# Constant products ahead of the first turn, one column tile, block 2's and 3's squares at other slices, FFN1's first left sums seven slices later

## The chip, the cores and the metric

The kernel runs on one core of one Trainium2 chip. The metric is the device time of one execution in microseconds (us). Before the change three runs took 2862.64, 2865.20 and 2865.36 us (median 2865.2). One execution was also recorded by the hardware profiler, instruction by instruction; every number about single instructions comes from that record, and its times count from the first instruction.

The engines are called as in the profile: PE (matrix products), PEld (its weight loads), DVE (vector), ACT (scalar and activation), POOL (general), SP (which issues DMAs). Each works through its own queue in the order in which it was written; an instruction that waits holds everything behind it on the same engine.

## What is computed

One layer of a transformer-like trunk: 2048 tokens of 1024 numbers, float32. Shift, scale and gate come from a conditioning vector c.

```python
mod_all = einsum('bd,lde->lbe', silu(c), ada_w) + ada_b
h = rms_norm(x, g0) * (1 + sc_m) + sh_m
y = stick_breaking_mixer(h, w_qkv, w_o)      # 16 heads of 64, causal, blocks of 128
x = x + gt_m * rms_norm(y, g1)
h = rms_norm(x, g2) * (1 + sc_f) + sh_f
g, u = split(h @ w_in); y = (silu(g) * u) @ w_out   # width 2816
x = x + gt_f * rms_norm(y, g3)
```

The mixer computes, per head, z = q k^T / 8, a weight for every earlier position as the product of sigmoid(z) with all sigmoid(-z) between, and the weighted sum of the values.

## The kernel before, in words

Float32 products are made of three fast ones: every operand is split into a high part (a cast on ACT, or POOL) and a low part (the difference, on DVE or POOL), and `mm3` (lines 176 to 180) multiplies high by high, high by low and low by high.

**Order.** PE, ACT, DVE and POOL run in the order in which the program is written; SP's DMAs are ordered by the framework. The unit of the order is a slice: one call of `mm3`, three products of 512 columns. The 2048 tokens are four blocks of 512, the 16 heads eight pairs. The projections are a list of steps, `STEPS`: pair 0 with block 0, pair 1 with block 0 (parked in memory), then pair 0 with blocks 1, 2, 3, and so on. A step has a key product (t = 1), a query product (t = 0) and a value product (t = 2), each of eight slices k = 0 to 7, then two empty slices. Step 2 is pair 0, block 1; step 3 is pair 0, block 2.

**The start** (lines 774 to 937, written out by hand). The first 2 x 1024 modulation numbers come in eight tiles m of 128, shift and scale each. A tile's `ada` weights are loaded by `row_load(m)`. Tiles 0 and 1 are multiplied on PE (`column`, line 699: eight products of one column per half, into `acol`); tiles 2 to 7 on DVE (`row_sum`, line 707: weights times `c_rows` with a running sum), where `c_rows` is silu(c) spread over all partitions by two products of a constant matrix. `row_done` (line 715) adds the bias. Block 0's x is normed by rows (`x_square`, `x_scale`), turned by PE (`turn_x`), modulated on ACT (`full`), split (`high`, `low`) and multiplied at once for pairs 0 and 1 (`products`).

**Blocks 1 to 3 of x** come already turned (`cols_load`), four loads of 512 KB each. Block 1's norm is taken from rows. For blocks 2 and 3, `cols_square` (line 315) squares the four loads on ACT, `cols_add` (line 323) adds them on DVE, m = 1, 2, 3 and a closing add of 512; for block 3 all squares from m = 1 on use the same buffer, so each waits for the add before it. `cols_sum` (line 330) sums over partitions with four products of one column and makes the root on POOL; `x_spread` (line 343, DVE) and `x_share` (line 350: four turns on PE, then a copy on ACT to the tile `xv`) lay the scales out as a row. `first_norm` (line 406) then scales (`scale_cols`; odd tiles on POOL), modulates and splits tile by tile, and stores each pair of tiles (1024 KB, `h_s`). In `project` (line 443) the tables `XSQUARE_AT`, `XADD_AT`, `XSUM_AT` say at which slice of the step before each of these is written. In step 2 this is block 2's work, in step 3 block 3's.

**Attention** starts in step 2's value product: `score` on PE into three banks (`z`), two sigmoids on ACT, `break_sticks` on DVE and POOL, turns on PE, `split_high` on ACT, `split_low` on DVE, and the product with the values. Its slots alternate with projection slices.

**FFN1** (lines 1531 to 1580): 44 groups, two halves of the tokens by 22; a group is seven products of four slices, a Strassen-like scheme. The left matrices of a group are sums of raw weights, made in the group before: `left_add` (line 1331, DVE) and `left_split` (line 1345, ACT and DVE). `ADD_AT` and `SPLIT_AT` give their slices; for the group after groups 0 and 22, where the right matrices of a half are still being split as well, `ADD_LATE` and `SPLIT_LATE` do, counted from the start of group 0 or 22. `taken` (line 1482) reads each product from its bank; line 1498 adds product 7 into `up1`, and product 4 goes on in the same bank after that. Raw weights of a group are loaded two groups ahead (`left_load`), into the buffers of the group that was just split.

Of the kernel before, what the change touches and what calls it, by code (L numbers as in the profile page):

```python
# [9 lines left out]
F32 = mybir.dt.float32  # L10
# [28 lines left out]

COLUMNS = 2  # L40

# [65 lines left out]
def hybrid_trunk_kernel(  # L107
# [215 lines left out]
    def cols_add(b, m):  # L323
        total = x_squares[b][0]
        if m < KC // 2:
            nc.vector.tensor_tensor(total, total, x_squares[b][m], op=ALU.add)
        else:
            nc.vector.tensor_tensor(total[:, 0], total[:, 0], total[:, 1], op=ALU.add)
# [21 lines left out]
    def x_share(b):  # L350
        spread = x_spreads.pop(b)
        pool, tag = (tps, "t") if b < 2 else (accps, "acc")
        pt = pool.tile([P, BT], F32, name=f"xr{b}", tag=tag)
        for i in range(4):
            nc.tensor.transpose(pt[:, i * P : (i + 1) * P], spread[:, i], ident)
        x_row[b] = att.tile([P, BT], F32, name=f"xv{b}", tag="tmp", bufs=BUFS["tmp"])
        nc.scalar.copy(x_row[b], pt)

    def x_scale(i):
        nc.vector.tensor_scalar(x_norm[i], x_tiles.pop((0, i)), x_rstd.pop((0, i)), None, op0=ALU.mult)  # L360
# [82 lines left out]
    def project(at):  # L443
# [10 lines left out]
        def product(t):  # L454
# [7 lines left out]
            for k in range(KC):  # L462
                if t == 1:
                    if p == 0:
                        first_norm(b, k + (4 if b == 1 else 3))
                    if k in (3, 5) and waiting:
                        waiting.pop(0)()
                if nb == 2 and (t, k) == (1, 4):
                    cols_load(3)
                if nb:  # L470
                    if (t, k) in XSQUARE_AT[nb]:
                        cols_square(nb, XSQUARE_AT[nb][t, k])
                    if (t, k) in XADD_AT[nb]:
                        cols_add(nb, XADD_AT[nb][t, k])
                    if (t, k) in XSUM_AT[nb]:
                        (cols_sum, x_spread, x_share)[XSUM_AT[nb].index((t, k))](nb)
                if (t, k) in NORM_AT:
# [207 lines left out]
    def row_load(m):  # L685
# [9 lines left out]
        for seg in range(2):  # L695
            src = ada_cols_first[m, seg] if m < COLUMNS else ada_rows[m - COLUMNS, seg]
            nc.sync.dma_start(halves_of[seg], src)
# [17 lines left out]
    def row_done(m):  # L715
        total = acol[:, 2 * m : 2 * m + 2] if m < COLUMNS else sums.pop(m)
        nc.vector.tensor_tensor(mod[:, :, m], total, b_cols[:, 0:2, m], op=ALU.add)
# [29 lines left out]
    def turn_x(m):  # L747
        turned_x[m] = x_turn(m)
# [25 lines left out]
    first_h, first_full, stores, turned_x = norm_h[0], {}, [], {}  # L774
    acol = zps.tile([P, BT], F32, name="acol", tag="z")
    c_line = att.tile([P, D], F32, name="c_line", tag="qkn", bufs=BUFS["qkn"])
# [25 lines left out]
    c_spread = [zps.tile([P, BT], F32, name=f"cs{half}", tag="z") for half in range(2)]  # L802
    c_halves = [slice(half * BT, (half + 1) * BT) for half in range(2)]
    for half in range(2):
        nc.tensor.matmul(c_spread[half], ones, c_line[:, c_halves[half]], start=True, stop=True)
    column(0, 0)
    column(0, 1)
    x_square(0, 0)
    for i in range(1, 4):
        x_square(0, i)  # L810
        x_scale(i - 1)
    c_rows = att.tile([P, D], F32, name="c_rows", tag="qkn", bufs=BUFS["qkn"])
    for half in range(2):
        nc.scalar.activation(c_rows[:, c_halves[half]], c_spread[half], AF.Sigmoid)
    x_scale(3)
# [3 lines left out]
    row_done(0)  # L819
    weights_high(0, 1)  # L820
# [3 lines left out]
    low(0)  # L824
    for half in range(2):
        nc.vector.tensor_tensor(
            c_rows[:, c_halves[half]], c_spread[half], c_rows[:, c_halves[half]], op=ALU.mult
        )
    products(0, 0, 1)
    column(1, 0)  # L830
# [10 lines left out]
    turn_x(2)  # L841
    products(0, 0, 2)
    weights_low(1, 1)
    for t in (1, 0, 2):
        first_acc[1, t] = zps.tile([P, BT], F32, name=f"pj1_0_{t}", tag="z")
    products(1, 0, 1)
    low(1)
    row_sum(2, 0)
    weights_high(1, 0)
    row_sum(2, 1)  # L850
    row_done(2)
    products(0, 1)
    weights_low(1, 0)
    products(1, 1, 1)
    full(2)
    high(2)
    weights_high(1, 2)
    products(1, 0, 0)
    row_sum(3, 0)
    weights_low(1, 2)  # L860
    turn_x(3)
    products(1, 1, 0)
    low(2)
    x_load(1, 0)
    x_load(1, 1)
# [900 lines left out]
```

## Time and profile before

| | |
|---|---|
| runs | 2862.64, 2865.20, 2865.36 us |
| profiled execution | 2863.12 us, span 2860.8 us |
| mean granted PE clock | 0.992 of full speed |
| PE busy | 2803.4 us of the span |
| DVE, ACT, POOL busy | 2032.0, 1633.3, 1284.1 us |
| FFN1's products | 1583.3 to 2433.0 us |

A line of the timeline has the start in us, the length in us, engine, line of the kernel, operation, what it writes and reads, its shape, and in brackets the idle time of the engine before it and what ended that. A window has busy time and number of instructions of each engine, the clock that PE was granted (1.00 is full), the share of time in which the 16 DMA engines were busy, and GB/s. A group has count, busy time and mean ns of one, then idle time before. L178, L179 and L180 are the three products of `mm3`, wherever they are called from.

### The profile page before, as it was taken

What the parts mean: (1) busy time and instruction counts of PE and PEld (TensorE: products, weight loads), DVE (VectorE), ACT (ScalarE), POOL (GpSimd) and SP (SyncE); (2) the same over time, 40 slices, a digit from 0 to 9 for tenths busy, and PEclk for the clock granted to TensorE, in tenths of its full rate; (3) what the DMA queues carried; (4) which work ended last, traced back from release to release, by engine and by line L of the source; (5) the groups of instructions that cost most, each with busy time, mean ns of one, the idle gap of its engine ahead of it and who ended that gap; (6) DMA issues with size and microseconds to landing.
All of it is one profiled execution on the core that took longest, in us unless ns stands there. A gap on an engine that the chain in (4) does not pass through costs nothing.

```text
span 2860.8 us, 41725 instructions
## 1 busy us (share of the span) xinstructions
PE 2803.4 (98%) x13809; PEld 2339.3 (82%) x13809; DVE 2032.0 (71%) x2827; ACT 1633.3 (57%) x3269; POOL 1284.1 (45%) x2030
## 2 busy tenths in 40 slices
PE   8799999999999999999999999999999999999998
PEld 7588888888888888887887888888788888888887
DVE  6788888888888888888866866555776655134376
ACT  5587777788787777877644533333433333322233
POOL 0475666667576665656410222212222222644454
PEclk8899999999999999999999999999999999999999
DMA  9665547666576545637289645334554335545566
GB/s 361 233 227 162 169 159 239 190 194 225 168 233 200 173 149 174 202 119 247 63 306 307 212 139 158 109 93 152 158 164 120 111 95 174 190 132 153 181 214 199
DMA packets 239209, 518.94 MB, mean 181 GB/s; under 512 B 22417, under 2 KB 108433, under 8 KB 222098
## 3 DMA queue, kind: packets, MB, share of 16 engines
q1 hardware_dynamic: 238994, 516.28, 55.8%
q8 instruction: 109, 1.79, 0.3%
q14 instruction: 106, 0.87, 0.1%
HBM read 348.95 MB, written 118.49 MB: 163 GB/s over the span
## 4 chain that ended last, share of the span: by engine, by line
PE 87%; DVE 4%; ACT 2%; issue 1%; DMA 1%; POOL 1%; SPq 0%; DVEq 0%; POOLq 0%; ACTq 0%
PE s L178 9%; PE s L180 9%; PE s L179 9%; PE z L588 8%; PE o L667 8%; PE t L639 8%; PE pj L178 5%; PE pj L180 5%; PE pj L179 5%; PE o L180 5%; PE o L178 5%; PE o L179 5%; PE y L180 2%; PE y L178 2%; PE y L179 2%
## 5 line engine op out<-in xcount | busy, mean ns | idle before, releaser
L629 POOL TENSOR_TENSOR a<-a,w 128x512 f32<-128x512 f32 (+3 forms) x640 | 622.2, 972 | 220.4 <-DVE w L622 130.9
L622 DVE TENSOR_TENSOR_SCAN w<-z,c,begin 128x512 f32<-128x512 f32 x384 | 489.2, 1278 | 83.6 <-ACT z L607 61.8
L178 PE MATMUL s<-r,l 128*128 128x512 f32 x1232 | 481.6, 391 | 4.7 <-DVE p L1498 4.4
L180 PE MATMUL s<-r,l 128*128 128x512 f32 x1232 | 479.5, 389 | 0.0
L179 PE MATMUL s<-r,l 128*128 128x512 f32 x1232 | 479.4, 389 | 0.0
L605 ACT ACTIVATE a<-z 128x512 f32<-128x512 f32 (+3 forms) x640 | 347.0, 542 | 168.3 <-PE z L588 136.8
L667 PE MATMUL o<-aT,v 128*128 128x512 f32 (+3 forms) x1280 | 385.0, 382 | 0.1
L655 DVE TENSOR_TENSOR aT<-t,aT 128x512 fp32r<-128x512 f32 (+3 forms) x640 | 358.5, 594 | 25.8 <-ACT aT L649 25.3
L588 PE MATMUL z<-kt,qt 128*128 128x512 f32 (+3 forms) x1280 | 363.9, 365 | 0.0
L649 ACT CAST aT<-t 128x512 fp32r<-128x512 f32 (+3 forms) x640 | 313.8, 533 | 79.6 <-PE t L639 69.6
L607 ACT ACTIVATE z<-z 128x512 f32<-128x512 f32 (+3 forms) x640 | 345.4, 540 | 0.0
L1506 POOL TENSOR_TENSOR one<-p,p 128x512 f32<-128x512 f32 x44 | 70.9, 1611 | 577.6 <-issue 320.6
L178 PE MATMUL pj<-ht,w 128*128 128x512 f32 x768 | 310.9, 405 | 4.8 <-issue 1.4
L639 PE MATMUL t<-begin,a 128*128 128x128 f32 x2176 | 296.1, 274 | 15.9 <-DVE aT L655 14.7
L639 PEld LDWEIGHTS t<-begin,a 128*128 128x128 f32 x2176 | 256.1, 141 | 66.5 <-DVE aT L655 17.2
L179 PE MATMUL pj<-ht,w 128*128 128x512 f32 x768 | 304.0, 396 | 3.8 <-DVE ht L387 2.3
L180 PE MATMUL pj<-ht,w 128*128 128x512 f32 x768 | 304.3, 396 | 0.1
L178 PEld LDWEIGHTS s<-r,l 128*128 128x128 f32 x1232 | 231.2, 188 | 55.0 <-DVE p L1498 3.0
L179 PEld LDWEIGHTS s<-r,l 128*128 128x128 f32 x1232 | 231.3, 188 | 48.4 <-issue 0.5
L180 PEld LDWEIGHTS s<-r,l 128*128 128x128 f32 x1232 | 231.2, 188 | 48.2
L617 DVE TENSOR_TENSOR_SCAN w<-z,begin 128x128 f32<-128x128 f32 (+3 forms) x256 | 208.5, 817 | 78.6 <-ACT z L607 66.6
L588 PEld LDWEIGHTS z<-kt,qt 128*128 128x128 f32 x1280 | 231.2, 189 | 37.6 <-DVE w L617 0.2
(180 smaller groups left out, 4885.9 us busy)
## 6 DMA issues: line engine op xcount, KB each, us to landing
ht<-h_s SPq DMA_DIRECT2D x108, 1024.0 KB, 8.2
wi<-in_win SPq DMA_DIRECT2D x86, 512.0 KB, 4.0
qt<-qn SPq DMA_DIRECT2D x124, 256.0 KB, 4.8
ol_qt<-act_s SPq DMA_DIRECT2D x56, 512.0 KB, 3.7
act_s<-S SPq DMA_DIRECT2D x66, 256.0 KB, 4.0
br<-in_wout SPq DMA_DIRECT2D x66, 256.0 KB, 3.5
h_s<-ht SPq DMA_DIRECT2D x16, 1024.0 KB, 6.9
o_s<-os SPq DMA_DIRECT2D x128, 128.0 KB, 2.9
```

Of the source, the lines that this page charges most:

```text
L178: nc.tensor.matmul(acc, lhs[0], rhs[0], start=first, stop=False, **kw)
L179: nc.tensor.matmul(acc, lhs[0], rhs[1], start=False, stop=False, **kw)
L180: nc.tensor.matmul(acc, lhs[1], rhs[0], start=False, stop=last, **kw)
L588: nc.tensor.matmul(z[:, :n], q[:, e, part, r * P : (r + 1) * P], k[:, e, :n], start=part == 0, stop=part == 1,)
L605: nc.scalar.activation(a[:, :n], z[:, :n], AF.Sigmoid, scale=QK_SCALE)
L607: nc.scalar.activation(z[:, :n], z[:, :n], AF.Sigmoid, scale=-QK_SCALE)
L622: nc.vector.tensor_tensor_scan(rest[:, rev], left[:, rev], begin[:, :BT][:, rev], initial=carries[r], op0=ALU.mult, op1=ALU.bypass,)
L629: nc.gpsimd.tensor_tensor(a[:, :n], a[:, :n], rest[:, 1 : n + 1], op=ALU.mult)
L639: nc.tensor.transpose(pt[:, rb * P : (rb + 1) * P], weighed[i, rb][:, j * P : (j + 1) * P], ident)
L649: nc.scalar.copy(hl[:, 0, t0:], pt[:, t0:])
L655: nc.vector.tensor_tensor(hl[:, 1, t0:], pt[:, t0:], f32(hl[:, 0, t0:]), op=ALU.subtract)
L667: nc.tensor.matmul(acc[:, t0:], lhs, hl[:, part, t0:], start=sc == qb and j == 0 and part == 0, stop=sc == 0 and j == 3 and part == 1,)
```

## The change

1. **Constant products.** `warm(n)` issues n products of a constant matrix with zeros, 384 columns each, into an unused bank: three ahead of the products that spread c, eleven behind them (before block 0 is turned), and one behind each half of tile 1's columns.
2. **Tile 0 by rows.** Tile 0 is now summed on DVE like tiles 2 to 7; tile 1 alone stays on PE. The two products c times its sigmoid move up, ahead of the second scaling of x. Other calls of the start change places: `row_sum(2, 0)` and the products of pair 0 ahead of `row_done(1)`, `row_sum(3, 0)` later.
3. **Block 1's row of scales** stays in its bank and is read there; the copy on ACT goes.
4. **Blocks 2 and 3.** One table gives the slice of every part. Block 2: squares 0 to 3 from (1,2), (1,3), (1,6), (1,7) to (1,3), (1,4), (1,5), (1,6); sum, spread and share from (0,2), (0,3), (0,5) to (0,5), (0,6), (2,0). Block 3's loads from (1,4) to (1,1) of step 2; its squares from step 3's (1,4), (1,5), (0,0), (0,2) to step 2's (2,3), (2,5) and step 3's (1,0), (1,3); its adds lie between; sum, spread and share from (0,5), (0,6), (0,7) to (0,1), (0,2), (0,6). Three adds of 1024 (block 2 m = 1, block 3 m = 1 and 2) go from DVE to POOL.
5. **FFN1.** `ADD_LATE` and `SPLIT_LATE` are seven slices later.

```diff
-COLUMNS = 2
+BY_COLUMNS = 1
...
-XSQUARE_AT = {2: {(1, 2): 0, (1, 3): 1, (1, 6): 2, (1, 7): 3}, 3: {(1, 4): 0, (1, 5): 1, (0, 0): 2, (0, 2): 3}}
-XADD_AT = {2: {(1, 5): 1, (1, 7): 2, (0, 0): 3, (0, 1): 4}, 3: {(1, 7): 1, (0, 1): 2, (0, 3): 3, (0, 4): 4}}
-XSUM_AT = {2: [(0, 2), (0, 3), (0, 5)], 3: [(0, 5), (0, 6), (0, 7)]}
+X_AT = {
+    (2, 1, 1): [("load", 3)],
+    (2, 1, 3): [("square", 2, 0)],
+    (2, 1, 4): [("square", 2, 1), ("add", 2, 1)],
+    (2, 1, 5): [("square", 2, 2)],
+    (2, 1, 6): [("square", 2, 3), ("add", 2, 2)],
+    (2, 1, 7): [("add", 2, 3)],
+    (2, 0, 0): [("add", 2, 4)],
+    (2, 0, 5): [("sum", 2)],
+    (2, 0, 6): [("spread", 2)],
+    (2, 2, 0): [("share", 2)],
+    (2, 2, 3): [("square", 3, 0)],
+    (2, 2, 5): [("square", 3, 1)],
+    (2, 2, 7): [("add", 3, 1)],
+    (3, 1, 0): [("square", 3, 2)],
+    (3, 1, 2): [("add", 3, 2)],
+    (3, 1, 3): [("square", 3, 3)],
+    (3, 1, 5): [("add", 3, 3)],
+    (3, 1, 6): [("add", 3, 4)],
+    (3, 0, 1): [("sum", 3)],
+    (3, 0, 2): [("spread", 3)],
+    (3, 0, 6): [("share", 3)],
+}
+ON_GPSIMD = ((2, 1), (3, 1), (3, 2))
...
-            nc.vector.tensor_tensor(total, total, x_squares[b][m], op=ALU.add)
+            engine = nc.gpsimd if (b, m) in ON_GPSIMD else nc.vector
+            engine.tensor_tensor(total, total, x_squares[b][m], op=ALU.add)
...
+        if b == 1:
+            x_row[b] = pt
+            return
...
+    idle = zps.tile([P, BT], F32, name="idle", tag="z")
+    def warm(n):
+        for _ in range(n):
+            nc.tensor.matmul(
+                idle[:, : BT - P], ones, begin[:, : BT - P], start=True, stop=True, skip_group_check=True
+            )
...
+    warm(3)
     for half in range(2):
         nc.tensor.matmul(c_spread[half], ones, c_line[:, c_halves[half]], start=True, stop=True)
-    column(0, 0)
-    column(0, 1)
+    warm(11)
     x_square(0, 0)
-    for i in range(1, 4):
-        x_square(0, i)
-        x_scale(i - 1)
+    x_square(0, 1)
+    x_scale(0)
...
+    x_scale(1)
+    x_square(0, 2)
+    row_sum(0, 0)
+    x_square(0, 3)
+    x_scale(2)
+    row_sum(0, 1)
     x_scale(3)
+    row_done(0)
...
     weights_low(0, 0)
+    warm(1)
     products(0, 0, 0)
     column(1, 1)
...
+    row_sum(2, 0)
+    warm(1)
+    products(0, 0, 2)
+    turn_x(2)
     row_done(1)
...
-    ADD_LATE = {14: 5, 18: 6, 21: 3, 26: 7}
-    SPLIT_LATE = {16: 1, 18: 5, 21: 6, 25: 3, 32: 7, 35: 2, 40: 4}
+    ADD_LATE = {21: 5, 25: 6, 28: 3, 33: 7}
+    SPLIT_LATE = {23: 1, 25: 5, 28: 6, 32: 3, 39: 7, 42: 2, 47: 4}
```

More of the change, by code (lines that the diff above doesn't have):

```diff
@@ L355, in x_share @@
             nc.tensor.transpose(pt[:, i * P : (i + 1) * P], spread[:, i], ident)
+        if b == 1:
+            x_row[b] = pt
+            return
         x_row[b] = att.tile([P, BT], F32, name=f"xv{b}", tag="tmp", bufs=BUFS["tmp"])
         nc.scalar.copy(x_row[b], pt)
+    x_do = {
+        "load": cols_load, "square": cols_square, "add": cols_add, "sum": cols_sum,
+        "spread": x_spread, "share": x_share,
+    }
     def x_scale(i):
@@ L467, in product @@
                         waiting.pop(0)()
[L468 to L476, printed above, removed]
+                for what, *which in X_AT.get((at, t, k), []):
+                    x_do[what](*which)
                 if (t, k) in NORM_AT:
@@ L824, in hybrid_trunk_kernel @@
     low(0)
[L825 to L828, printed above, removed]
     products(0, 0, 1)
+    acol = zps.tile([P, BT], F32, name="acol", tag="z")
     column(1, 0)
```

26 lines of the change are left out of this document (13 added, 13 removed).

## The prediction, made before the changed kernel was run

> **What bounds the kernel now.** The page comes first: the span, and how much of it the engines work.
>
> ```profile
> span 2860.8 us, 41725 instructions
> PE 2803.4 (98%) x13809; PEld 2339.3 (82%) x13809; DVE 2032.0 (71%) x2827; ACT 1633.3 (57%) x3269; POOL 1284.1 (45%) x2030
> ```
>
> TensorE (PE) is idle for 2860.8 - 2803.4 = 57.4 us. The windows of PE alone say where. Columns: stretch, length, busy, granted clock, DMA share, GB/s.
>
> ```profile
> 0.00:50.00 50.00, 41.54 (x180) 0.83 0.96 379
> 50.00:100.00 50.00, 42.36 (x191) 0.93 0.99 350
> 100.00:150.00 50.00, 38.28 (x182) 0.86 0.41 134
> ```
>
> 27.8 us of the idle time lie in the first 150 us, where the clock is low too. The change touches that stretch and two boundaries in FFN1 (last part of the working); their waits are what it can be worth. Next, the timeline of PE (start, length, line, tiles, idle time before and what ended it) and windows of all engines (PE, weight loads, DVE, ACT, POOL, clock, DMA): three at half clock and one of undisturbed work.
>
> ```profile
> 17.80 0.80 PE L178 MATMUL pj<-ht,w 128*128 128x512 f32 x1 [0.67 <-ACT ht L763]
> 76.98 1.86 PE L334 MATMUL xq<-ones,xs 128*128 128x1 f32 x8 [4.41 <-DVE xs L328]
> 91.78 0.62 PE L588 MATMUL z<-kt,qt 128*128 128x512 f32 x2
> 97.17 0.50 PE L179 MATMUL pj<-ht,w 128*128 128x512 f32 x1 [1.15 <-DVE ht L394]
> 100.45 0.79 PE L179 MATMUL pj<-ht,w 128*128 128x512 f32 x1 [2.31 <-DVE ht L387]
> 105.49 0.40 PE L178 MATMUL pj<-ht,w 128*128 128x512 f32 x1
> 111.56 0.33 PE L639 MATMUL t<-begin,a 128*128 128x128 f32 x1 [2.73 <-DVE aT L655]
> 118.81 1.86 PE L334 MATMUL xq<-ones,xs 128*128 128x1 f32 x8 [4.15 <-DVE xs L328]
> 125.56 0.48 PE L178 MATMUL pj<-ht,w 128*128 128x512 f32 x1
> ```
>
> ```profile
> 15.01:32.08 17.07, 16.41 (x62) 14.31 (x62) 9.57 (x15) 6.77 (x8) 0.00 (x0) 0.50 1.03 409
> 78.70:83.28 4.58, 4.58 (x13) 3.60 (x14) 1.03 (x5) 0.00 (x0) 1.02 (x1) 0.50 1.01 406
> 118.81:124.24 5.43, 5.43 (x19) 4.74 (x20) 2.65 (x8) 0.00 (x0) 2.27 (x6) 0.50 0.01 2
> 2030.00:2045.00 15.00, 15.00 (x68) 12.42 (x67) 12.21 (x20) 8.31 (x15) 0.41 (x1) 1.00 0.33 105
> ```
>
> In the undisturbed window a product starts every 15.00 / 68 = 0.22 us, and a slice of three takes 0.66. PE waits twice for a sum of squares (4.41 and 4.15 us) and each time runs on at half clock; between, it waits for block 2's operands (1.15, 2.31) and for a low half of a turned tile (2.73). Slices are named as in the code: (t, k) with t = 1 for keys, 0 for queries, 2 for values; step 2 is pair 0 with block 1, step 3 pair 0 with block 2. Three rows are my marks: the fourth score product of the attention at 91.78, (1,7) of step 3 at 105.49 and (0,7) of step 3 at 125.56.
>
> **The start (constant products, tile 0 by rows).** The timeline (PE and weight loads) and one window of PE:
>
> ```profile
> 7.36 3.75 PE L805 MATMUL cs<-c_line,ones 128*128 128x512 f32 x4 [7.36 <-DMA c_line<-in_c_row]
> 11.45 3.80 PEld L703 LDWEIGHTS acol<-c_act,ar 128*128 128x128 f32 x32 [1.91 <-DVE n_ms L171]
> 14.00:15.00 1.00, 1.00 (x12) 1.00 1.02 414
> ```
>
> In the row at 7.36 two products of 512 columns take 3.75 us, so a constant one of 384 takes 1.41 like that, and half, 0.70, at full clock (the row at 14 shows it; the stretch from 15.01 is at half). Three stand ahead of 7.36, where PE is idle anyway: nothing. Eleven follow from 7.36 + 3.75 = 11.1: with full clock at once they end at 18.8, with two slow ones at 20.3. Tile 0's columns (3.80 on PE) go; two row sums of 128x1024 (2.4 us, as two adds of 1.20 below) come on DVE behind the earlier sigmoids, beside the constant products; its load only changes its source, not its size. Before, the first product came 17.80 - (11.45 + 3.80) = 2.6 us after the columns ended. The same behind the constant products is 21.4 to 22.9: 3.6 to 5.1 late. From there PE may have full clock where it had half for 32.08 - 17.80 = 14.3 us (7.1 us back), or lose it again, since one-column products dropped it at 15.01 and two remain, each with only one constant product behind it. I take nothing for all this, between 3.5 us of gain and 5.1 of loss, because the next part has a floor that doesn't depend on it. Block 1's row of scales is read from PSUM, which saves a copy of 0.6 on ACT and may cost its eight readers 0 to 0.1 each: nothing.
>
> **Block 2's sum and the loads of block 3.** The sum moves three slices on, so 2.0 of the 4.41 us are filled with work. One add of block 2 moves to POOL, idle there: up to 1.2 us longer (2.40 against 1.20, rows below), started as soon as its square is there, so nothing. The sharing moves three slices on with it. What is late next? Block 3's data: four loads of 512 KB (cols_load(3)) are issued three slices earlier, past one 1024 KB store of h_s on SP; the squares of block 3 that read them move from step 3's (1,4), (1,5) to step 2's (2,3), (2,5). The tile view of xc on SP, the DMA view at 72 to 82 us, and rows of ACT and DVE:
>
> ```profile
> L305 SPq DMA_DIRECT2D xc<-in_xt x4: 781/1207/1264, 76.1 to 79.5; - x4
> DMA to landing us min/median/max: 12.3/12.6/13.1
> DMA packets 703, 4.26 MB, mean 426 GB/s; under 512 B 80, under 2 KB 80, under 8 KB 286
> 88.36 0.80 ACT L391 ACTIVATE xc<-xc,mod,g_eff 128x512 f32<-128x512 f32 x1
> 90.45 0.42 DVE L617 TENSOR_TENSOR_SCAN w<-z,begin 128x128 f32<-128x128 f32 x1
> ```
>
> The loads land from 76.1 + 12.3 = 88.4 on. DMA is full, so only the store put behind them helps: 1.05 MB / 426 GB/s = 2.5 us, to 85.9. However early PE arrives, ACT stands at the first square of block 3 until then: its whole queue (norms of block 2, sigmoids) waits, and with three banks PE gets no further than the fourth score product. After the square (1.06, row below) follows what took 90.45 + 0.42 - 88.36 = 2.5 us: 85.9 + 1.06 + 2.5 = 89.5 instead of 91.78, a gain of 2.3. If SP keeps the old order, the gain is 0.
>
> **Block 3's chain.** Squares 2 and 3 reuse one buffer, so each waits for the add before it. Those adds (m = 1, 2) move to POOL. Rows of the timeline, and one group:
>
> ```profile
> 109.49 1.06 ACT L321 ACTIVATE xs<-xc 128x1024 f32<-128x1024 f32 x1 [2.24 <-issue]
> 113.14 1.20 DVE L326 TENSOR_TENSOR xs<-xs 128x1024 f32<-128x1024 f32 x1
> L206 POOL TENSOR_TENSOR w<-wr,w 128x1024 fp32r<-128x1024 f32 x21 | 50.4, 2399 | 0.0
> 94.47 0.87 POOL L629 TENSOR_TENSOR a<-a,w 128x384 f32<-128x384 f32 x1 [0.72 <-DVE w L617]
> 95.30 1.27 POOL L379 TENSOR_TENSOR xc<-xc,xv 128x512 f32<-128x512 f32 x1
> 98.40 1.45 POOL L629 TENSOR_TENSOR a<-a,w 128x512 f32<-128x512 f32 x1 [1.79 <-DVE w L617]
> 99.81 1.72 POOL L379 TENSOR_TENSOR xc<-xc,xv 128x512 f32<-128x512 f32 x1
> 94.65 0.62 ACT L392 CAST ht<-xc 128x512 fp32r<-128x512 f32 x1
> 95.30 1.82 DVE L394 TENSOR_TENSOR ht<-xc,ht 128x512 fp32r<-128x512 f32 x1 [0.40 <-ACT ht L392]
> ```
>
> An add of 1.20 on DVE is about 2.40 on POOL (the L206 shape). POOL is in order: from 91.5 (2 us after the fourth score product) add, weigh, scale, weigh, scale, add: 2.40 + 0.87 + 1.27 + 1.45 + 1.72 + 2.40 = 10.1, to 101.6. ACT stands at square 3 until then, and behind it is block 2's last norm: 1.06 + 0.80 + 0.62 (its cast) to 104.1, and (1,7) runs at about 104.5 against 105.49. So 1.3 of the 2.3 us are given back: ACT's hold takes the place of the waits of 1.15 and 2.31. An idle stretch before (1,7) costs some half clock behind it: 2.0, a little under half of the 4.58 above.
>
> From (1,7) to (0,7) it was 125.56 - 105.49 = 20.1 us. ACT no longer stands at 109.49, so the 2.73 go; the 4.15 go; half of the 5.43 at half clock goes: 20.1 - 2.7 - 4.2 - 2.7 = 10.5. New: the sum is read at (0,1), four slices sooner, with two adds just issued on DVE (1 us of wait), the sharing (1 us, its three small steps on DVE and POOL were 2 us and have four slices), and the 2.0: 14.5. (0,7) comes at 104.5 + 14.5 = 119.0, a gain of 6.6. The two 1s are estimates from 0 to 2. What follows is the old work at the old pace.
>
> The Trainium skill, page SBUF — State Buffer, section Who interferes with whom, says that a DVE instruction with two SBUF inputs and a reading GpSimd instruction exclude each other for a whole instruction. The trace agrees: the L394 above took 1.82 beside a POOL scale of 1.27 that began with it, and 1.82 - 1.27 is about the 0.6 that such an operation needs. By that rule the adds on POOL would shut DVE out also, and the sum would come out like the second rival below.
>
> **FFN1.** The waits of PE in 1980 to 2160 and 1480 to 1700, and DVE's timeline:
>
> ```profile
> PE s L178 <- DVE p L1498: 3.1, 2, 2.6
> PE s L178 <- DVE p L1498: 0.9, 1, 0.9
> 2019.58 0.68 DVE L1342 TENSOR_TENSOR ls<-wi 128x512 f32<-128x512 f32 x1
> 2026.29 0.68 DVE L1498 TENSOR_TENSOR p<-s,p 128x512 f32<-128x512 f32 x1
> ```
>
> PE waits 2.6 us for the sum L1498 in group 22, and 0.9 in group 0. DVE is behind there: two sums and two splits of the next left matrix (the first one shown and three more between it and L1498, 0.6 us each) are queued ahead. Seven slices later they come behind it: L1498 is 2.4 us earlier. Gain 2.2 and 0.8, together 3.0. The cost: the same work in the next group, with 2.4 us more ahead of a due time of 5 to 8 slices (3.3 to 5.3 us), and the raw weights two groups on are loaded up to 7 x 0.66 = 4.6 us later. Both are covered; if not, the 3.0 is given back: 0 to 3.
>
> **The sum.** The profiled execution took 2863.1 with its span of 2860.8. 2863.1 - 6.6 - 3.0 = 2853.5. The runs shown have a median of 2865.2 and reach from 0.5 below to 2.2 above that execution, so I forecast 2855.
>
> **The rivals.** First, the slower one: POOL holds block 2's norms. Place: step 3, (1,3) to (1,7). With a total gain of 9.6 it decides from (1,7) at 104.5 + 9.6 = 114.1 on, and makes the kernel 0.2% slower from 119.8.
>
> ```profile
> L1068 POOL TENSOR_TENSOR of<-op 128x512 f32<-128x512 f32 x8 | 11.8, 1476 | 0.2 <-DMA op<-o_s 0.2
> ```
>
> At its upper end an add is two of these, 2.95; if each holds first ACT and then DVE, in series, two cost 11.8, and two stretches of half clock 4.0: (1,7) at 120.3, and 2868 to 2870. For it: PE already waits for these norms (1.15, 2.31). Against it: the holds overlap.
>
> Second: POOL's adds shut DVE out as the scale did in the row of 1.82, so DVE, whose queue PE waits for here, saves nothing: each add costs 2.40 where it saved 1.20, and the half clock comes twice: 2 x 1.2 + 2.0 more, 2857 to 2859. The exclusion on the Trainium skill's page SBUF — State Buffer is this case.
>
> Third, the change doesn't do what it says at the start: ACT stands at landings of 88.4, the chain ends as late as before, and only FFN1 gives its 3.0: 2860 to 2862.
>
> Fourth, the holds do not show, because POOL is through before ACT gets there: (1,7) 5 us sooner, 2848.
>
> **How the numbers follow.** 0.2%, some 5.7 us, is about what a measurement of this kernel can tell from no change. Chances: my forecast 0.42 (its own range 2851 to 2859), the fourth 0.12, the second 0.17 (two thirds of it still faster by 0.2%), the third 0.17, the slower one 0.12. Faster 0.42 + 0.12 + 0.11 = 0.65; within 0.2%: 0.06 + 0.17 = 0.23; slower 0.12. The range 2847 to 2866 leaves out the slower rival and the end of the fourth.
>
> **What would show it.** Right: the wait before block 2's sum under 3 us and no half clock after it; ACT idle at the first square of block 3 until about 86; the fourth score product near 89.5, (1,7) near 104.5, (0,7) near 119; no wait over 0.5 us for L1498 in groups 0 and 22. Wrong: a PE wait over 4 us in step 3's (1,3) to (1,7), a wait for block 3's sum at (0,1) as long as the old one, or waits for left matrices in groups 1 and 23.

## The result, and the profile after

| | before | changed |
|---|---|---|
| median of the runs (6 each) | 2862.1 us | 2852.0 us (2849.8 to 2855.7) |
| profiled execution, span | 2863.1, 2860.8 us | 2851.9, 2849.8 us |
| fourth score product | 91.78 | 88.86 |
| (1,7) of step 3 | 105.49 | 107.59 |
| (0,7) of step 3 | 125.56 | 118.73 |
| FFN1, first to last product | 849.7 | 846.1 |

The changed kernel takes 0.9965 of the time before, 95% interval 0.9952 to 0.9977: about 10 us faster. The forecast was 2855. The 11.0 us between the two spans lie here: 6.8 at (0,7); 0.6 lost between there and FFN1 (a wait at 1541 us for a normed x, 2.48 against 1.95); 3.6 in FFN1; 1.2 in the code after FFN1, which was not changed and took 426.6 to 428.4 us over all the runs below.

From the page of the changed kernel, and from its windows of PE (stretch, length, busy, granted clock, DMA share, GB/s):

```profile
span 2849.8 us, 41730 instructions
PE 2802.1 (98%) x13809; PEld 2334.5 (82%) x13809; DVE 2027.4 (71%) x2828; ACT 1633.5 (57%) x3268; POOL 1289.5 (45%) x2033
```

```profile
0.00:50.00 50.00, 45.84 (x203) 1.00 0.96 380
50.00:100.00 50.00, 38.90 (x169) 0.90 1.00 342
100.00:150.00 50.00, 42.29 (x208) 0.90 0.56 193
```

PE is idle for 47.7 us instead of 57.4. Of these 150 us the first 50 are at full clock (0.83 before), the last 50 have 4 us more work in them; the middle stretch is worse than before. The timeline of PE, at the places that the prediction marked (line numbers are now those of the changed file; L198 to L200 are `mm3`):

```profile
17.94 0.49 PE L198 MATMUL pj<-ht,w 128*128 128x512 f32 x1 [1.08 <-ACT ht L785]
51.32 0.49 PE L376 MATMUL xr<-begin,xw 128*128 128x128 f32 x3
72.62 0.61 PE L355 MATMUL xq<-ones,xs 128*128 128x1 f32 x4 [2.68 <-DVE xs L349]
88.86 1.22 PE L610 MATMUL z<-kt,qt 128*128 128x512 f32 x2 [4.62 <-DVE w L639]
99.77 0.50 PE L199 MATMUL pj<-ht,w 128*128 128x512 f32 x1 [2.33 <-DVE ht L416]
104.22 0.80 PE L199 MATMUL pj<-ht,w 128*128 128x512 f32 x1 [1.12 <-DVE ht L416]
107.59 0.44 PE L198 MATMUL pj<-ht,w 128*128 128x512 f32 x1
109.72 1.02 PE L355 MATMUL xq<-ones,xs 128*128 128x1 f32 x8 [0.38 <-DVE xs L349]
118.73 0.39 PE L198 MATMUL pj<-ht,w 128*128 128x512 f32 x1
```

The waits for the two sums fell from 4.41 and 4.15 to 2.68 and 0.38, and the 2.73 for a low half is gone. A new wait of 4.62 stands before the fourth score product. Its releaser is a scan on DVE, but behind that scan stands ACT's queue, held at block 3's loads; and later ACT and DVE are held again, by POOL's second add. (ACT's row at 103.65 names L624, a small fill that POOL runs as the add ends; the square starts when the add is through, at 100.81 + 2.81 = 103.62.) Rows of ACT, POOL and DVE:

```profile
85.34 1.06 ACT L341 ACTIVATE xs<-xc 128x1024 f32<-128x1024 f32 x1 [4.08 <-DMA xc<-in_xt]
103.65 1.06 ACT L341 ACTIVATE xs<-xc 128x1024 f32<-128x1024 f32 x1 [4.44 <-POOL w L624]
105.44 0.62 ACT L421 CAST ht<-xc 128x512 fp32r<-128x512 f32 x1
```

```profile
91.80 2.38 POOL L347 TENSOR_TENSOR xs<-xs 128x1024 f32<-128x1024 f32 x1
94.30 1.16 POOL L651 TENSOR_TENSOR a<-a,w 128x384 f32<-128x384 f32 x1
100.81 2.81 POOL L347 TENSOR_TENSOR xs<-xs 128x1024 f32<-128x1024 f32 x1
```

```profile
101.66 2.51 DVE L416 SCALAR_TENSOR_TENSOR ht<-xc,mod,ht 128x512 fp32r<-128x512 f32 x1
```

Between 1980 and 2160 us PE waits for one sum, 0.5 us at the end of that stretch, as before; the two waits of 0.92 and 2.61 for the sum (L1498, now L1535) are gone.

### The profile page after: what moved, and what is told of

Same layout as the page of the kernel before. It is cut to its first block, busy times and chain, and to the rows that moved or that the text cites. A ratio compares the mean times of both kernels' runs of the same rounds, so it can differ in the third digit from the quotient of the medians.

```text
span 2849.8 us, 41730 instructions
## 1 busy us (share of the span) xinstructions
PE 2802.1 (98%) x13809; PEld 2334.5 (82%) x13809; DVE 2027.4 (71%) x2828; ACT 1633.5 (57%) x3268; POOL 1289.5 (45%) x2033
## 4 chain that ended last, share of the span: by engine, by line
PE 86%; DVE 4%; DMA 3%; issue 2%; ACT 2%; POOL 1%; SPq 0%; DVEq 0%; POOLq 0%; ACTq 0%
PE s L198 9%; PE s L200 9%; PE s L199 9%; PE z L610 8%; PE o L689 8%; PE t L661 8%; PE pj L198 5%; PE pj L199 5%; PE pj L200 5%; PE o L199 5%; PE o L198 5%; PE o L200 5%; PE y L200 1%; PE y L198 1%; PE y L199 1%
## 5 line engine op out<-in xcount | busy, mean ns | idle before, releaser
L198 PE MATMUL s<-r,l 128*128 128x512 f32 x1232 | 481.5, 391 | 1.2 <-DVE p L1535 0.7
L200 PE MATMUL s<-r,l 128*128 128x512 f32 x1232 | 479.6, 389 | 0.0
L198 PE MATMUL pj<-ht,w 128*128 128x512 f32 x768 | 310.2, 404 | 6.0 <-issue 1.4
L661 PE MATMUL t<-begin,a 128*128 128x128 f32 x2176 | 296.3, 274 | 13.5 <-DVE aT L677 12.3
L200 PE MATMUL pj<-ht,w 128*128 128x512 f32 x768 | 302.7, 394 | 0.0
L198 PEld LDWEIGHTS s<-r,l 128*128 128x128 f32 x1232 | 231.3, 188 | 51.2 <-DVE p L1535 1.5
L200 PEld LDWEIGHTS s<-r,l 128*128 128x128 f32 x1232 | 231.3, 188 | 48.6 <-DVE l L1397 0.4
```

The source lines that it names most:

```text
L198: nc.tensor.matmul(acc, lhs[0], rhs[0], start=first, stop=False, **kw)
L200: nc.tensor.matmul(acc, lhs[1], rhs[0], start=False, stop=last, **kw)
L661: nc.tensor.transpose(pt[:, rb * P : (rb + 1) * P], weighed[i, rb][:, j * P : (j + 1) * P], ident)
```

## The experiments

Three kernels do one part of the change each; the others take a part away, move squares, or add constant products. The marks below are PE's, in us of each profiled execution; "turn" is the turning of block 1's scales, the end of the start. The last column is the ratio to the kernel before on the same chip, with its 95% interval.

| kernel | turn | 4th score | (1,7) | (0,7) | span | median | ratio |
|---|---|---|---|---|---|---|---|
| before | 56.03 | 91.78 | 105.49 | 125.56 | 2860.8 | 2862.1 | |
| changed | 51.32 | 88.86 | 107.59 | 118.73 | 2849.8 | 2852.0 | 0.9965 (0.9952 to 0.9977) |
| FFN1 alone | 59.75 | 95.61 | 109.37 | 129.43 | 2859.3 | 2857.8 | 0.9978 (0.9968 to 0.9988) |
| blocks alone | 57.13 | 92.08 | 109.36 | 124.89 | 2857.9 | 2858.5 | 0.9980 (0.9971 to 0.9988) |
| start alone | 59.28 | 94.80 | 108.58 | 127.68 | 2861.2 | 2859.2 | 0.9984 (0.9975 to 0.9993) |
| adds on DVE | 52.16 | 90.96 | 107.02 | 120.67 | 2847.9 | 2849.8 | 0.9947 (0.9935 to 0.9960) |
| changed, again | 59.20 | 92.78 | 111.50 | 122.65 | 2849.5 | 2851.7 | 0.9957 (0.9944 to 0.9969) |
| no constant products | 57.76 | 92.45 | 109.72 | 122.33 | 2850.5 | 2852.7 | 0.9963 (0.9950 to 0.9975) |
| last square later | 53.03 | 89.61 | 107.17 | 118.72 | 2847.3 | 2849.4 | 0.9955 (0.9942 to 0.9967) |
| squares later | 58.77 | 90.75 | 106.14 | 123.05 | 2850.7 | 2852.8 | 0.9962 (0.9949 to 0.9976) |
| five constant products | 52.52 | 90.27 | 107.52 | 123.05 | 2851.3 | 2850.2 | 0.9953 (0.9939 to 0.9966) |
| five, squares later | 52.19 | 84.13 | 99.28 | 116.39 | 2843.7 | 2846.1 | 0.9944 (0.9931 to 0.9957) |
| five, last square later | 53.98 | 89.83 | 106.98 | 118.33 | 2846.7 | 2848.7 | 0.9946 (0.9934 to 0.9959) |

### Each part alone

FFN1 alone, in the kernel before:

```diff
-    ADD_LATE = {14: 5, 18: 6, 21: 3, 26: 7}
-    SPLIT_LATE = {16: 1, 18: 5, 21: 6, 25: 3, 32: 7, 35: 2, 40: 4}
+    ADD_LATE = {21: 5, 25: 6, 28: 3, 33: 7}
+    SPLIT_LATE = {23: 1, 25: 5, 28: 6, 32: 3, 39: 7, 42: 2, 47: 4}
```

> The kernel before, with only the two tables of FFN1 seven slices later. My theory: the start and the blocks on one side and FFN1 on the other add up, and FFN1 gives what its two waits for the sum in group 0 and group 22 were, 0.92 + 2.61 = 3.5 us: 3.0 to 3.7 us faster than before. Rival: most of the 3.5 us comes back as waits for the left matrices of groups 1 and 23, or at the end of FFN1, and the gain of the whole change came from the blocks: 0 to 1 us faster. In the trace: no wait of PE for that sum between 1480 and 1700 or 1980 and 2160 us; by the rival, new waits over 0.5 us in the group behind.

Measured: 0.9978, that is 6.3 us faster by the ratio, between 3.4 and 9.2. Both waits are gone. Counted from a group's first product to that of the next, group 0 is shorter by 20.93 - 19.69 = 1.2 us and group 22 by 21.93 - 19.42 = 2.5. Little of it comes back: no wait over 0.4 us came in group 1 or 23, and group 23 takes 19.31 instead of 19.05. A wait of 1.12 in the last group, the end of FFN1 of which the rival speaks, stands in this profile alone; the nine others with the new tables have 0.5 or less there. So the rival is out. In the blocks alone and the start alone, where the old tables stand, group 22 took 23.20 and 23.42 instead of 21.93: the clock fell behind the wait. A window of the blocks alone and the same window of FFN1 alone:

```profile
2024.00:2028.00 4.00, 4.00 (x13) 0.62 0.22 66
```

```profile
2024.00:2028.00 4.00, 3.89 (x18) 1.00 0.00 0
```

13 products in 4 us against 18, at a clock of 0.62. So the wait of 2.5 costs 2.5 in some executions and 3.8 to 4.0 in others, and FFN1's term is 3.7 to 5.2 by these two groups. The whole of FFN1 takes 849.7 to 851.1 us in the three profiles with the old tables and 845.6 to 847.0 in the ten with the new.

The blocks alone (the kernel before with `X_AT` and `ON_GPSIMD` in place of the three old tables):

```diff
-XSQUARE_AT = {2: {(1, 2): 0, ...
-XADD_AT = ...
-XSUM_AT = ...
+X_AT = { ... }
+ON_GPSIMD = ((2, 1), (3, 1), (3, 2))
...
```

> The kernel before, with only the table of blocks 2 and 3 and the three adds on POOL; start and FFN1 as before. My theory: the loads of block 3 are the floor, so the five microseconds that the new start wins by 51 us are worth nothing behind them: ACT stands at the first square of block 3 until 85 to 87, the fourth score product is within 1.5 us of 88.9, and the kernel is 5.5 to 7 us faster than before. Rival: the start's lead is needed, since with it gone PE gets to block 3's squares after the loads have landed: the fourth score product at 91 to 93 and a gain of 1 to 3 us.

Measured: 0.9980, 5.7 us faster (3.4 to 8.3): the size of my theory, and not the rival's. But its reason is not the one I gave. The fourth score product came at 92.08, where only the rival had it, and ACT didn't stand at block 3's loads at all: PE got there later than the loads. The columns turn and (0,7) say more: the turning came 57.13 - 51.32 = 5.8 us later than in the changed kernel, (0,7) 124.89 - 118.73 = 6.2 later. Between these two executions the start's lead wasn't lost up to (0,7). And the 5.7 us rest on the times of its eleven runs: in its profile (0,7) comes only 125.56 - 124.89 = 0.7 us sooner than in the kernel before, and the span is 2.9 us shorter.

The start alone (the changed kernel with the three old tables and FFN1 as before):

```diff
-X_AT = { ... }
-ON_GPSIMD = ((2, 1), (3, 1), (3, 2))
+XSQUARE_AT = {2: {(1, 2): 0, ...
+XADD_AT = ...
+XSUM_AT = ...
...
-    ADD_LATE = {21: 5, 25: 6, 28: 3, 33: 7}
+    ADD_LATE = {14: 5, 18: 6, 21: 3, 26: 7}
...
```

> The changed kernel with blocks 2 and 3 and FFN1 as before: constant products, tile 0 by rows and block 1's row read from its bank are left of the change. My theory: PE is some 5 us ahead at 51 us, then waits longer for block 2's sum or for ACT at block 3's loads, which land at 88 us as before; the fourth score product stays within 1 us of 91.8 and the time within 1.5 us of before. Rival: the lead is kept through blocks 2 and 3, (0,7) of step 3 comes at 120 to 122, and the kernel is 4 to 5 us faster.

Measured: 0.9984, 4.6 us faster (2.0 to 7.2), so the start is worth something with the old blocks, on average over its runs. Its profile shows none of that: the turning came at 59.28, later than before. The reason is in the next part. The three gains don't add up: 6.3 + 5.7 + 4.6 = 16.6, where the whole change gave 10.0 and, measured again, 12.3. FFN1 and the blocks make 12.0 of that by themselves, each known to some 2.5 us, so within the whole little is left for the start.

### The clock at the start

The same kernel was profiled twice:

> The changed kernel once more, for the same chip as the three beside it. If the start's full clock is a matter of where the clock's own steps fall, its profile shows products 0.23 us apart from 24 us on, as in the first profile of it, or 0.43 apart up to about 35 as in the run of the start alone; in the second case the keys' product of the last pair of block 0 and the turning of block 1's scales (51.3 us at first) come 5 to 7 us later. Time between 0.9952 and 0.9977 of before.

Its time was 2851.7, ratio 0.9957, as in the first measurement. Its start was another. The timeline of PE in the first profile, the products that spread c (L835) and then from the first columns of tile 1 on (L725 columns, L801 constant products):

```profile
6.94 1.96 PE L835 MATMUL cs<-c_line,ones 128*128 128x512 f32 x4 [1.48 <-DMA c_line<-in_c_row]
...
19.24 1.84 PE L725 MATMUL acol<-c_act,ar 128*128 128x1 f32 x16
20.94 0.89 PE L801 MATMUL idle<-begin,ones 128*128 128x384 f32 x2
...
25.04 0.40 PE L199 MATMUL pj<-ht,w 128*128 128x512 f32 x1
25.28 0.39 PE L200 MATMUL pj<-ht,w 128*128 128x512 f32 x1
```

and in the second:

```profile
7.41 3.75 PE L835 MATMUL cs<-c_line,ones 128*128 128x512 f32 x4 [1.89 <-DMA c_line<-in_c_row]
...
21.47 0.49 PE L198 MATMUL pj<-ht,w 128*128 128x512 f32 x1 [1.08 <-ACT ht L785]
...
22.77 2.47 PE L725 MATMUL acol<-c_act,ar 128*128 128x1 f32 x16
25.09 1.63 PE L801 MATMUL idle<-begin,ones 128*128 128x384 f32 x2
...
27.80 3.41 PE L725 MATMUL acol<-c_act,ar 128*128 128x1 f32 x16
...
32.92 0.63 PE L199 MATMUL pj<-ht,w 128*128 128x512 f32 x1
33.34 0.63 PE L200 MATMUL pj<-ht,w 128*128 128x512 f32 x1
```

Sixteen columns take 1.84 us at first; in the second profile they slow down to 2.47 while they run, the next sixteen take 3.41, and a product starts 0.42 us after the one before instead of 0.24. The turning comes at 59.20 instead of 51.32. With one constant product behind each half of the columns the clock was kept in three profiles (changed, adds on DVE, last square later: turning at 51.3 to 53.0) and lost in three (changed again, start alone, squares later: 58.8 to 59.3). The Trainium skill, page TensorE: Matmul & The Clock Gate, section What's actually happening, says that the window over which the activity is watched runs free of the kernel's start; that fits one program that falls either way. The start ahead of the columns differs too. Of the nine profiles with constant products, the four in which the spreading took 1.95 or 1.96 us all kept the clock; of the five in which it took 2.73 to 3.75 three lost it.

What the constant products are worth was tried by leaving them out:

```diff
     def warm(n):
-        for _ in range(n):
+        for _ in range(0):
```

> The changed kernel without the constant products (they compute nothing that is used); tile 0 is still summed on DVE. By my prediction the start is worth nothing behind the loads of block 3: within 1.5 us of the changed kernel. Rival, which the first runs speak for (in the blocks alone, 5.8 us later at the turning of block 1's scales meant 6.2 later at (0,7) of step 3): the lead is kept, so that without constant products, with the clock lost until 32 us, the kernel is 4 to 6 us slower than the changed one.

Measured: 2852.7 against 2851.7, ratios 0.9963 and 0.9957. That is 1.0 us, too little for the measurement to tell from nothing, and nothing of the 4 to 6 of the rival. Its (0,7), at 122.33, is 0.3 us sooner than in the second profile of the changed kernel and 3.6 later than in the first. Where does the lead go? From the two profiles of the changed kernel: 59.20 - 51.32 = 7.9 us of lead at the turning are 3.9 at the fourth score product and 3.9 at (0,7). Half is lost where ACT stands at block 3's loads: 4.08 us in the first profile, 0.2 in the second. The loads are issued at 74.7 in the one and 77.3 in the other, so they move, but by a third of the lead only.

The other half doesn't reach the end either: the spans are 2849.8 and 2849.5. FFN1 starts at 1577.08 in the first profile and at 1577.27 in the second, so 0.2 us of the 3.9 are left there. Most of the loss lies at one wait of PE for a normed x, and behind it (first profile, then second):

```profile
1541.43 0.47 PE L1082 MATMUL h2T<-begin,x1n 128*128 128x128 f32 x1 [2.48 <-DVE x1n L1075]
```

```profile
1543.08 0.33 PE L1082 MATMUL h2T<-begin,x1n 128*128 128x128 f32 x1 [1.40 <-DVE x1n L1075]
```

Behind the longer wait two products start 0.43 us apart (1543.41 and 1543.84), behind the shorter one 0.22 (1543.49 and 1543.71). DVE makes that x behind a step that waits for ACT, and ACT stands there at a load from `h_s`, until 1539.00 and until 1540.63. So a lead at (0,7) is not yet a gain.

Two runs test what happens at block 3's loads. The first has five constant products instead of two around the columns, as below; the second, in the next part, moves the squares away from the loads as well.

```diff
     turn_x(0)
     turn_x(1)
+    warm(2)
     weights_high(0, 1)
...
-    warm(1)
+    warm(2)
     products(0, 0, 0)
...
-    warm(1)
+    warm(2)
     products(0, 0, 2)
```

> The changed kernel with five constant products where it has two: two more ahead of the first product and two instead of one behind each half of tile 1's columns (1.3 us of PE time each pair). If the clock at the start is lost only in executions in which the one-column products fall into one of the clock's own steps with too little else, it is now kept: products 0.23 us apart from 26 us on, the turning of block 1's scales by 53 to 55 us, and ACT stands 2 to 4 us at the first square of block 3. The time then is that of the lucky executions of the changed kernel, 2847 to 2850, in nearly all runs (0.5 to 3 us below its median). Rival: the clock is lost all the same, by the waits rather than by the columns, and the longer queue costs 1 to 3 us more: 2852 to 2855.

The clock was kept in its profile and in the two others that have these products (turning at 52.2 to 54.0). Three of three beside three of six doesn't prove that the five products keep it, the less as two of these three had the spreading of c at 1.95 and 1.96. The median is 2850.2, a little above the 2847 to 2850 that I expected of nearly all runs; they reach from 2848.2 to 2853.5, four of the five above 2850 and two of them in the rival's range. So the start is not the only thing that varies, or it isn't kept in all of them. Its own profile shows another: (0,7) only at 123.05, with a wait of 3.27 for the fourth score product and a loss behind (1,7) that is told below.

### What the lead runs into

Block 3's squares in step 3, behind the loads, with the adds on DVE (first alone, then with the five constant products):

```diff
-    (2, 2, 3): [("square", 3, 0)],
-    (2, 2, 5): [("square", 3, 1)],
-    (2, 2, 7): [("add", 3, 1)],
-    (3, 1, 0): [("square", 3, 2)],
-    (3, 1, 2): [("add", 3, 2)],
-    (3, 1, 3): [("square", 3, 3)],
-    (3, 1, 5): [("add", 3, 3)],
-    (3, 1, 6): [("add", 3, 4)],
-    (3, 0, 1): [("sum", 3)],
-    (3, 0, 2): [("spread", 3)],
+    (3, 1, 0): [("square", 3, 0)],
+    (3, 1, 1): [("square", 3, 1)],
+    (3, 1, 2): [("add", 3, 1)],
+    (3, 1, 3): [("square", 3, 2)],
+    (3, 1, 4): [("add", 3, 2)],
+    (3, 1, 5): [("square", 3, 3)],
+    (3, 1, 6): [("add", 3, 3)],
+    (3, 1, 7): [("add", 3, 4)],
+    (3, 0, 2): [("sum", 3)],
+    (3, 0, 3): [("spread", 3)],
...
-ON_GPSIMD = ((2, 1), (3, 1), (3, 2))
+ON_GPSIMD = ()
```

> Adds on DVE, and block 3's squares at (1,0), (1,1), (1,3), (1,5) of step 3 with the adds between, sum at (0,2). If it is the stand of ACT at block 3's loads that keeps PE waiting before the fourth score product (4.6 us in the changed kernel, 6.5 with the adds on DVE), that wait falls under 1 us and the product comes at 85 to 86. What is won at (0,7) of step 3: 2 to 4 us over the changed kernel if block 2's norms follow, 0 if ACT's later squares hold them as the early ones did (waits of PE of 2 us or more in (1,3) to (1,7)), less than nothing if the sum at (0,2) becomes the wait.

> Both: the five constant products, and block 3's squares in step 3 with the adds on DVE. If the lead of the start is eaten by ACT's stand at block 3's loads, it now gets through: no wait of PE over 1.5 us before the fourth score product, which comes at 84 to 87 us, (0,7) of step 3 at 115 to 117.5 and the time 2845 to 2848. Rival: the next thing that the lead runs into is as late (block 2's norms on DVE and POOL, the sum at (0,2)): (0,7) at 118 to 120 and no gain over the five constant products alone.

The first lost its clock at the start (turning at 58.77), came to the fourth score product without a wait and ended at 2852.8: nothing won. The second kept it, and its timeline shows the wait of 4.62 gone:

```profile
52.19 0.49 PE L376 MATMUL xr<-begin,xw 128*128 128x128 f32 x3
84.13 0.62 PE L610 MATMUL z<-kt,qt 128*128 128x512 f32 x2
93.07 0.79 PE L199 MATMUL pj<-ht,w 128*128 128x512 f32 x1 [2.33 <-DVE ht L416]
105.17 1.84 PE L355 MATMUL xq<-ones,xs 128*128 128x1 f32 x8 [3.18 <-DVE xs L349]
116.39 0.39 PE L198 MATMUL pj<-ht,w 128*128 128x512 f32 x1
```

Between these two kernels a lead of 6.58 us at the turning is 6.62 at the fourth score product and 6.66 at (0,7): with ACT's stand at the loads out of the way, all of it gets through, where the changed kernel lets half of it through. Here it is in the span as well, 7.0 us. (0,7) at 116.39 and the median of 2846.1 are as expected, though two of the five runs took 2850.7 and 2851.7. At 0.9944 (0.9931 to 0.9957) this version beats the kernel before, and its median is the lowest of all; that it beats the changed kernel (0.9957 and 0.9965) its (0,7) and its median suggest, but the intervals overlap. Block 3's sum is read too early at (0,2): PE waits 3.18 us for it.

### POOL's adds

The three adds back on DVE, in the changed kernel:

```diff
-ON_GPSIMD = ((2, 1), (3, 1), (3, 2))
+ON_GPSIMD = ()
```

> The changed kernel with the three adds back on DVE. My theory: POOL's two adds for block 3 hold ACT at square 3 (4.4 us) and through it block 2's last norm, so (1,7) of step 3 came 3.1 us later than I forecast; on DVE each add takes 1.2 instead of 2.4 to 2.8 us, ACT stands 2 to 3 us less, (1,7) comes 1 to 3 us sooner, and the kernel is 1 to 3 us faster than the changed one. Rival: DVE's own queue is what PE waits for here (low halves of block 2), and three adds in it push those back by as much: 1 to 3 us slower than the changed one, (1,7) at 108.5 to 111. Third: both at once, within 1 us.

Measured: 0.9947 (0.9935 to 0.9960); the changed kernel had 0.9965 and 0.9957, so the median is 2 us better, and the intervals overlap. The rival that adds on DVE cost 1 to 3 us is not borne out. In the trace both things happen. The fourth score product comes 2.1 us later than in the first profile of the changed kernel (90.96, with a wait of 6.50; block 3's first square runs at 87.44 instead of 85.34, behind its load). Yet (1,7) is 0.6 sooner. From the fourth score product to (1,7) it takes 16.1 us instead of 18.7: the second wait for DVE falls from 1.12 to 0.30, and ACT's stand at the last square from 4.44 to 3.35:

```profile
104.23 1.06 ACT L341 ACTIVATE xs<-xc 128x1024 f32<-128x1024 f32 x1 [3.35 <-DVE xs L347]
```

But from (1,7) to (0,7) it takes 13.6 instead of 11.1, because PE now waits 1.29 for the sum of block 3 instead of 0.38 and loses the clock. Together 29.7 and 29.9: up to (0,7), and in these two profiles, POOL's adds cost what they save. (0,7) itself is 1.9 us later and the span 1.9 us shorter, so the better median isn't explained by these marks.

Is it ACT's stand at the last square that makes (1,7) late? The square one slice later, behind block 2's last norm, alone and with the five constant products:

```diff
-    (3, 1, 3): [("square", 3, 3)],
+    (3, 1, 4): [("square", 3, 3)],
```

> The changed kernel with the last square of block 3 one slice later, behind block 2's last norm on ACT instead of ahead of it. By my step (POOL's add holds ACT, ACT holds the last norm) the last low half comes 3 to 4 us sooner, the wait of 1.1 us before (1,6) goes and (1,7) comes 2 to 4 us sooner (104 to 106); the time falls by 1 to 3 us if the sum at (0,1) doesn't take it back. Rival: DVE, shut out by the same add, is late anyway, and nothing changes: (1,7) within 1 us of 107.6.

> The five constant products, and only the last square of block 3 one slice later. The last square later gained 1.2 us between the fourth score product and (1,7), and 0.8 up to (0,7), in its first run: if that was no accident of the clock, (0,7) comes 0.5 to 1.5 us sooner than with the five constant products alone. Rival: no difference within 0.5 us at (0,7).

In the first, ACT's stand there is 1.30 instead of 4.44, as it should be, and yet (1,7) came at 107.17, within the rival's 1 us of 107.6. The reason is in DVE's and POOL's rows of that kernel:

```profile
102.48 2.51 DVE L416 SCALAR_TENSOR_TENSOR ht<-xc,mod,ht 128x512 fp32r<-128x512 f32 x1
104.92 0.90 DVE L423 TENSOR_TENSOR ht<-xc,ht 128x512 fp32r<-128x512 f32 x1
```

```profile
101.64 2.80 POOL L347 TENSOR_TENSOR xs<-xs 128x1024 f32<-128x1024 f32 x1
```

The add runs from 101.64 to 104.44; the operation on DVE beside it takes 2.51 and ends half a microsecond after the add. The same operation in the kernel with the squares later, where no add is on POOL:

```profile
102.72 0.72 DVE L416 SCALAR_TENSOR_TENSOR ht<-xc,mod,ht 128x512 fp32r<-128x512 f32 x1
```

The exclusion of which the Trainium skill's page SBUF — State Buffer speaks (section Who interferes with whom) fits the add too: this DVE operation reads two operands from SBUF, and it is through only when the POOL instruction is. So there are two holds side by side, ACT behind the add and DVE beside it, and to take one away changes little: from the fourth score product to (1,7) 17.56 instead of 18.73, and with the five constant products 17.15 instead of 17.25. With the five constant products (0,7) came at 118.33, 4.7 us before the kernel without the later square, far more than the 0.5 to 1.5 expected, but the difference lies behind (1,7) (11.35 against 15.53), where the clock was kept in one execution and lost in the other. It proves nothing for the square. Windows of that stretch, in the first profile of the changed kernel and in that with five constant products:

```profile
107.59:118.73 11.14, 10.76 (x62) 1.00 0.57 189
```

```profile
107.52:123.05 15.53, 14.03 (x61) 0.78 0.43 137
```

The same 62 instructions (one record is missing) take 10.76 us of PE at full clock and 14.03 at 0.78. In front of them stands the wait for block 3's sum, 0.38 in the one and 1.28 in the other.

## Why the prediction was right, and where not

The time was right: 2855 forecast, 2852 measured, inside the range of the forecast's own case (2851 to 2859). The sum has two terms, and both parts were run alone: 6.6 for blocks 2 and 3 (alone 5.7 by its times) and 3.0 for FFN1 (alone 6.3, interval 3.4 to 9.2; in the first profile 3.6). The gain of 6.8 at (0,7) in the first profile looks like the 6.6, but 56.03 - 51.32 = 4.7 of it were there at the turning already, in the start that the sum puts at nothing. In the second profile (0,7) comes only 125.56 - 122.65 = 2.9 sooner, with the same span. So the total was right, and the mark at (0,7) confirms the term in one execution only. The steps:

- **The start, taken as 0.** The working had the first product at 21.4 to 22.9. The first profile shows 17.94, mainly because the spreading of c was already at full clock (two products in 1.96 us, not 3.75), so that the constant products ended at 16.0; the first product then came 1.9 behind them, not 2.6. The second profile shows 21.47, with the spreading at 3.75. The two outcomes that the working named for the clock behind it (kept, 7.1 back; or lost again) are both there, one in each. Lost, the turning comes at 58.8 to 59.3, 1 to 3 us behind most kernels without the constant products (56.0 to 57.8, once 59.75); kept, 3 to 6 ahead. Zero as a mean is near what the run without constant products says (1.0, with tile 0 still by rows) and what FFN1 and the blocks leave of the whole (12.0 against 10.0 and 12.3); the start with the old blocks is worth 4.6. So the term is mis-sized alone and nearly right in the change. That the two outcomes ended at the same time owes much to the wait at 1541 us, which the working doesn't have.
- **"The next part has a floor that doesn't depend on it."** This failed in part. Block 3's loads move with the start (74.7 against 77.3), and where PE comes late there is no stand at them at all. The floor takes about half of the lead by (0,7), not all; between the two profiles of the changed kernel the rest went behind (0,7), between the two with the squares later it stayed.
- **Block 2's sum**: 2.68 left of 4.41, as foretold (under 3). That no half clock would follow was wrong. It came, but for half as long as before (the turning of the scales at 77.3 is back at full clock):

```profile
74.55 0.63 PE L200 MATMUL pj<-ht,w 128*128 128x512 f32 x1
74.98 0.63 PE L198 MATMUL pj<-ht,w 128*128 128x512 f32 x1
...
78.65 0.39 PE L199 MATMUL pj<-ht,w 128*128 128x512 f32 x1
78.88 0.39 PE L200 MATMUL pj<-ht,w 128*128 128x512 f32 x1
```

- **Block 3's loads and the fourth score product** were right in the first profile: the first square ran at 85.34 (foretold 85.9), the product at 88.86 (89.5). The store was put behind the loads. In the second profile PE itself was late, and they came at 89.25 and 92.78.
- **(1,7) at 104.5** was wrong: 107.59. POOL's second add ended at 103.6 instead of 101.6. The list of what stands before it began 0.3 later (91.80), a weighing took 1.16 instead of 0.87, a wait of 1.0 for DVE was not in it, and the add took 2.81, not 2.40. Behind it the working had ACT's hold alone; DVE was shut out as well (2.51 in the place of 0.72), and PE had a mean clock of 0.70 from 98 to 105, behind its waits. The second rival's mechanism was there: in part, beside the hold, not instead of it.
- **From (1,7) to (0,7) in 14.5** was wrong the other way: 11.1. The wait for the sum was 0.38, not 1, the sharing made none, and no half clock followed. Other executions with the sum at (0,1) took 11.1 to 15.5. The two errors of 3.1 and 3.4 us cancel, and (0,7) came at 118.7 where 119.0 was foretold. That hit was luck.
- **FFN1's 3.0** was a little small: the traces give 3.7, and 1.3 to 1.5 more where the clock falls behind the wait of 2.5, which the sum did not count.

Of the rivals, the slower one did not come: (1,7) was 6.5 us short of the 114.1 from which it decides. "Nothing at the start, only FFN1" is refuted by the blocks alone. "The holds don't show" is refuted by (1,7) in every run that has POOL's adds. Two of the rivals' times are 1 to 2 us short if they are counted from the forecast: 5 us under 2855 is 2850, not 2848, and the slower one, 15.8 us later at (1,7), comes to 2871, not 2868 to 2870. Neither decides anything here.

What stays open: the wait at 1541 us for a normed x is 0 to 2.5 us over the runs, in no order that I can tie to an edit; ACT's stand at a load is behind it in both profiles of the changed kernel, but what sets its length is not shown. And why the clock is lost at the start in one execution and kept in another is shown only as far as the spreading and the columns; the phase itself was not tried.

## What to carry to other kernels

A stretch that was won counts only up to the next engine queue that stands on a transfer: look which instruction waits for the load, what is queued behind it, and move that instruction, not only the load. Where the clock is kept in one execution and lost in the next, one profiled execution is one draw: take differences between marks, follow them to the end of the kernel, and profile the same kernel twice before a term of 4 us is believed. Work moved to POOL can hold two-operand work on DVE for its whole length (2.51 us instead of 0.72 here), so price it at what it shuts out.

## What was not expected of the hardware

- One program kept the full clock at the start in one execution and lost it in the next (sixteen columns in 1.84 us, or in 2.47 and then 3.41), with 7.9 us between them at the end of the start. The longest wait of PE just ahead was 1.08 us in both.
- A wait of 2.5 us within otherwise full work left the clock alone in one execution and in two others cost 1.3 to 1.5 us of half clock besides.
- The granted clock of the records can miss this. In the profile of FFN1 alone the window from 20 to 30 us reads 1.00, yet it holds 37 products, fewer than the 41 that the kernel before has there at 0.50, and the changed kernel has 57. Sixteen columns take 3.41 us in it, as they do in the kernel before at 0.50. The spacing of the products is the safer reading:

```profile
20.00:30.00 10.00, 9.34 (x37) 1.00 1.03 410
```

```profile
20.00:30.00 10.00, 10.00 (x57) 1.00 1.03 409
```
